# Weights in SBUF places of 16 KB a partition, experts' weights in transfers of 2 MB

## The chip, the cores and the metric

The kernel runs on one core of a Trainium2 chip. The metric is the device time of one execution in microseconds (us). TensorE (PE) does the matmuls, VectorE (DVE) and ScalarE (ACT) the elementwise work, GpSimd (POOL) a few scans, and SyncE (SP) issues nearly all loads from HBM to SBUF. SBUF has 128 partitions; "8 KB a partition" is 1 MB in all. Sixteen DMA engines move the data.

## The reference

Three blocks work in a chain on one input `x` of 256 tokens by 1024 features, all in float32. The first has two layers of feed-forward networks (width 2816) around a mixer. The second has attention and then a mixture of 32 experts. The third has attention beside a state-space branch, a cross-attention to a memory of 1024 features, and a feed-forward network with a convolution. The experts are what the change is about. The reference, cut to that:

```python
def moe_ffn(h, w_router, b_router, w_mlp1, b_mlp1, w_mlp2, b_mlp2):
    logits = (xf @ w_router + b_router).astype(jnp.float32)
    top_val, top_idx = lax.top_k(logits, TOP_K)          # 4 of 32 experts
    gates = jax.nn.softmax(top_val, axis=-1)
    ...
    def expert_block(args):
        xb, e = args
        hid = xb @ w_mlp1[e] + b_mlp1[e]                 # 1024 x 2048
        glu = jnp.minimum(hid[..., ::2], SWIGLU_LIMIT)
        lin = jnp.clip(hid[..., 1::2], -SWIGLU_LIMIT, SWIGLU_LIMIT)
        act = glu * jax.nn.sigmoid(SWIGLU_ALPHA * glu) * (lin + 1.0)
        return act @ w_mlp2[e] + b_mlp2[e]               # 1024 x 1024
    ...
    y = y * slot_gate[:, None].astype(y.dtype)
    out = jax.ops.segment_sum(y, slot_tok, num_segments=n + 1)[:n]
```

An expert has 8 MB in `w_mlp1` and 4 MB in `w_mlp2`. All 32 experts get tokens, so 384 MB are read for them; the whole kernel reads 705 MB.

## The kernel before

The activations stay in SBUF in transposed form (`xT`: features on partitions, 8 blocks of 128 features by 256 tokens). A weight outside the experts is loaded into a place of 8 KB a partition, split by ACT (L181, `hi`) and DVE (L182, `lo`) into a high and a low part, and used by three matmuls each (`mm3`, L198 to L200). The splits go through a ring of 8 tiles, the loads through a pool of 10 places (`rawp`). `slot` (L311) hands out the next place of that pool, `raw` (L314) loads into it (L318). When a place is asked for again, the load waits until all readers of what lay there are done. SP issues the loads in the order of the program, so a load that waits holds up all that stand behind it.

The experts are used without the split. `moe` (L1264) takes them one by one in an order that the router gives. `weights` (L1299) issues 12 loads of 1 MB for each expert at L1294. Feature `8p + u` of the expert's input lies with partition `p`, so row `u` of `w_mlp1` is one contiguous piece of 8 KB for each partition (2048 numbers), and rows `u` and `u + 1` are neighbours in HBM. Of `w_mlp2` one load takes two rows of 1024 numbers, again 8 KB. The places for these loads come in a fixed cycle of 16 (L1284): seven of `rawp`, four of a pool of its own (`wb`), two that are lent (`input` and `xT`, which the experts don't need; `xT` is kept in HBM meanwhile and loaded back at L1776), and three of `rawp`. The first expert's last row goes to `xe`. The matmuls with `w_mlp1` stand at L1516 (half a block of tokens) and L1548 (a full one), those with `w_mlp2` at L1590; L1563 and L1575 turn the activations between them, L1603 adds the result into the output. A transfer counts on one of eight semaphores in turn, and a load waits until the transfer before it on the same semaphore has landed, so that eight are under way at most. At three turns of the loop, weights and memory for the third block's cross-attention are loaded in between (`mem.fetch`), and a loop at L1781 for experts with more tokens than the turns allow for runs no round here.

Of the kernel before, what the change touches and what calls it, by code (L numbers as in the profile page):

```python
# [12 lines left out]
F32 = mybir.dt.float32  # L13
# [6 lines left out]
P = 128  # L20
T = 256
D = 1024
KT = D // P
# [18 lines left out]
class Net:  # L42
    def __init__(self, ctx, tc, I):
        self.ctx, self.tc, self.nc, self.I = ctx, tc, tc.nc, I
        self.uid = 0
        pool = lambda name, bufs, **kw: ctx.enter_context(tc.tile_pool(name=name, bufs=bufs, **kw))
        self.const = pool("const", 1)
        self.psum = pool("psum", 8, space=PSUM)
        self.small = pool("small", 2)
        self.rawp = pool("rawp", 10, reuse_waits="tile")  # L50
        self.inputs = pool("inputs", 2, reuse_waits="tile")
        self.ring_size, self.ring_scope, self.right_scope, self.latest = None, None, None, ()
        self.rings(8)
        nc = self.nc
        self.ident = self.const.tile([P, P], F32, name="ident")
        make_identity(nc, self.ident)
        self.ones = self.const.tile([P, 1], F32, name="ones")
        nc.vector.memset(self.ones, 1.0)
        self.mhalf = self.const.tile([P, 4], F32, name="mhalf")
        nc.vector.memset(self.mhalf, -0.5)  # L60
        self.sc = self.const.tile([P, KT], F32, name="sc")
        self.xT = self.const.tile([P, KT, T], F32, name="xT")
        self.new_inputs()
# [86 lines left out]

    def load_x(self, ap):
        nc = self.nc
        xin = self.rawp.tile([P, 2, D], F32, tag="raw", name=self.nm("xin"))
        for q in range(2):
            c = slice(512 * q, 512 * q + 512)
            nc.sync.dma_start(xin[:, :, c], ap[:, c].rearrange("(h p) d -> p h d", p=P))
        for j in range(0, KT, 2):
            ps = self.bank()
            for z in range(2):
                for h in range(2):  # L160
                    nc.tensor.transpose(ps[:, z * T + h * P:z * T + (h + 1) * P], xin[:, h, (j + z) * P:(j + z + 1) * P], self.ident)
            nc.vector.tensor_copy(self.xT[:, j:j + 2, :].rearrange("p j t -> p (j t)"), ps)

    def store_x(self, ap):
        nc = self.nc
        for q in range(2):
            ot = self.rawp.tile([P, 2, 512], F32, tag="raw", name=self.nm("ot"))
            for h in range(2):
                ps = self.bank()
                for j in range(4):  # L170
                    nc.tensor.transpose(ps[:, j * P:(j + 1) * P], self.xT[:, 4 * q + j, h * P:(h + 1) * P], self.ident)
                if h:
                    nc.scalar.copy(ot[:, h, :], ps)
                else:
                    nc.vector.tensor_copy(ot[:, h, :], ps)
            nc.sync.dma_start(ap[:, q * 512:(q + 1) * 512].rearrange("(h p) d -> p h d", p=P), ot)
# [131 lines left out]
        return r[:, 0:2], r[:, 2:4]  # L308


    def slot(self, dtype=F32):  # L311
        return self.rawp.tile([P, 2048], dtype, tag="raw", name=self.nm("raw"))

    def raw(self, src, k, n, load=True):  # L314

# [5 lines left out]
    def unit(self, src, slot=False):  # L321

        hi, lo = self.parts(src.shape[1], src.shape[2], slot)
        self.latest = self.split(hi, lo, src)
        return hi, lo
# [944 lines left out]
    def moe(self, V, mod, router, w1, w2, b2, nxt, ahead, mem):  # L1270
# [5 lines left out]
        outer_pools, first_pools, first_products = ExitStack(), ExitStack(), ExitStack()  # L1276
        pool = lambda name, bufs=1, **side: outer_pools.enter_context(self.tc.tile_pool(name=self.nm(name), bufs=bufs, reuse_waits="tile", **side))
        top, p0, p6 = (pool(name, side="right") for name in ("mot", "mo0", "mo6"))
        p3, pb = pool("mo3", 4), pool("mob")

        own = lambda: p3.tile([P, 2048], F32, tag="wb", name=self.nm("wb"))


        lent = [self.input, lambda: self.xT.rearrange("p j t -> p (j t)")]  # L1284
        places = itertools.cycle([self.slot] * 7 + [own] * 4 + lent + [self.slot] * 3)

        def place(last=False):
            p = next(places)
            return next(q for q in itertools.chain([p], places) if not (last and q in lent))()

        def load(src, n, t):

            t = t.rearrange("p (k n) -> p k n", n=n)
            nc.sync.dma_start(t, src)  # L1294
            return t

        chosen_rows = lambda: px.tile([P, KT, T], F32, tag="xe", name=self.nm("xe")).rearrange("p k n -> p (k n)")

        def weights(a, b, other={}, late=False, last=False):  # L1299
            a = a.rearrange("(p k) n -> p k n", k=KT)  # L1300
            b = b.rearrange("(p k) n -> p k n", k=KT)
            if late:
                room = [self.slot() for _ in range(4)]
                return lambda u: load(a[:, u:u + 1, :], 2048, room[u % 4]), lambda u: load(b[:, 2 * u:2 * u + 2, :], D, room[u])
            wa = {u: load(a[:, u:u + 1, :], 2048, place(last)) for u in range(KT) if u not in other}
            wb = [load(b[:, 2 * u:2 * u + 2, :], D, place(last)) for u in range(4)]
            wa.update((u, load(a[:, u:u + 1, :], 2048, t())) for u, t in other.items())
            return wa, wb

# [21 lines left out]
        half = [r >= HALF or (c > 0 and ranks[c - 1] == r) for c, r in enumerate(ranks)]  # L1331
# [11 lines left out]
        b1 = pb.tile([P, 2, 512], F32R, name=self.nm("b1"))  # L1343
        nc.sync.dma_start(b1.bitcast(F32), self.b1)
        start = weights(w1[0], w2[0], {7: chosen_rows})
        tokens = self.input().rearrange("p (h k q) -> p h k q", h=2, k=KT)
        with self.tc.high_priority():
# [6 lines left out]
            with self.behind([self.powered]):  # L1354
# [5 lines left out]
                while c < N:  # L1360
                    r, n = ranks[c], 1
                    if r < FULL:
                        nc.gpsimd.memset(crow[:, c:c + 2], float(r))
                        nc.gpsimd.memset(skip[:, c + 1:c + 2], float(S))
                        n = 2
# [28 lines left out]
            for h in range(2):  # L1394
# [9 lines left out]
                last = nc.vector.tensor_scalar(mask[:, h, :], rep[:, :E], -2e38, None, op0=ALU.is_le).ins  # L1404
# [30 lines left out]
        last = nc.vector.tensor_scalar(perm, crow, rank[:, 1:2], None, op0=ALU.is_equal).ins  # L1435
# [6 lines left out]
        with self.behind([last]):  # L1442
            nc.vector.scalar_tensor_tensor(slot, pp[:, :2 * E].rearrange("p (h e) -> p h e", h=2), 1.0, mask, op0=ALU.add, op1=ALU.mult)

            for h in range(2):
                last = nc.vector.tensor_scalar(oh0[:, h, :], iot, 1.0, slot[:, h, 0:1], op0=ALU.add, op1=ALU.is_equal).ins
        with self.behind([last]):
            nc.vector.tensor_scalar(slot, slot, 1.0, None, op0=ALU.subtract)
            cnt = p0.tile([P, E], F32, name=self.nm("cnt"))
            nc.vector.tensor_copy(cnt, pp[:, 2 * E:3 * E])  # L1450
# [27 lines left out]
        with self.tc.tile_pool(name=self.nm("mo1"), bufs=1, reuse_waits="tile") as p1, \  # L1478
# [280 lines left out]
            for turn_, r in enumerate(order):  # L1759
                e = nc.sync.value_load(ids[0:1, c:c + 1], min_val=0, max_val=E - 1)  # L1760
                wa, wb = weights(w1[bass.ds(e, 1)].rearrange("o a n -> (o a) n"), w2[bass.ds(e, 1)].rearrange("o a n -> (o a) n"), last=turn_ == len(order) - 1)
                mine = [c, c + 1] if r < FULL else [c]
                c += len(mine)
                late = [n for n in range(3) if mem and turn_ == VALUES + 2 * n]
                for n in late:
                    mem.fetch("v", n)
                acts = first(mine, wa)
                if c < N and c not in got:
                    prepare(c)
                second(mine, [(turned_half if half[i] else turned)(a) for i, a in zip(mine, acts)], wb)  # L1770
                if turn_ == VALUES - 3:
                    bias()
                    ends, key, rest, at, eid, ecol4 = beyond()
                for n in late:
                    mem.value(n, lambda: p2.tile([P, 2, T], F32, tag="a", name=self.nm("mv")))
# [5 lines left out]
            with tc.For_i(0, count, 1):  # L1781
                who = p2.tile([P, 2], F32, tag="who", name=self.nm("who"))
                u = p2.tile([P, E], F32, tag="u", name=self.nm("u"))
# [4 lines left out]
                wa, wb = weights(w1[bass.ds(e, 1)].rearrange("o a n -> (o a) n"), w2[bass.ds(e, 1)].rearrange("o a n -> (o a) n"), late=True)  # L1788
# [4 lines left out]
                for h in range(2):  # L1793
                    u = p2.tile([P, E], F32, tag="u", name=self.nm("u"))
# [1082 lines left out]
```

## Time and profile before

| | us |
|---|---|
| median of 3 runs (lowest to highest) | 2651.24 (2647.99 to 2656.15) |
| the profiled execution | 2649.92 |
| its span in the trace | 2648.2 |
| PE busy in the span | 2416.1 (91%) |
| DVE busy, ACT busy | 1339.3 (51%), 915.4 (35%) |
| transfers for the experts, 1 MB each | 384 |

The profile divides the span into 40 slices of 66.2 us, counted from 0 here. The experts' work lies in slices 18 to 31 (about 1180 to 2130 us). The attention of the second block lies just before them, in slices 15 to 17, and the third block behind them. Line numbers are those of the kernel before. A list of waits gives the total in us, how often, and the longest. In a timeline, a row gives start, duration, engine, line, operation, tiles and count of merged instructions, and in brackets the idle time before with what ended it. A table of stretches gives the length, the busy time of PE, PEld (weight loads into TensorE), DVE, ACT and POOL with their counts of instructions, the mean granted clock of TensorE as a share of full speed, the mean busy share of the 16 DMA engines, and GB/s.

### The profile page before, as it was taken

The numbers are of one execution on the slowest core, as the hardware profiler recorded it, in microseconds if no ns is written. First come the engines' busy times: TensorE is split into PE (matmuls) and PEld (weight loads), VectorE is DVE, ScalarE is ACT, GpSimd is POOL, SyncE is SP. The second block draws the span as 40 slices with busy tenths as digits, with TensorE's granted clock in tenths as the row PEclk, the third lists the DMA queues.
The fourth block names the chain that finished last, engine by engine and source line by source line (L and its number), as shares of the span: only waits on it lengthen the run. The fifth ranks groups of instructions, "written<-read, shape, count | busy, mean of one in ns | idle before, by whom it ended". The sixth has DMA issues, their size and how long they took to land. (4 is left out here: it accounts for less than half of the span.)

```text
span 2648.2 us, 42809 instructions
## 1 busy us (share of the span) xinstructions
PE 2416.1 (91%) x17207; PEld 1833.3 (69%) x17207; DVE 1339.3 (51%) x2778; ACT 915.4 (35%) x1531; POOL 254.3 (10%) x444
## 2 busy tenths in 40 slices
PE   7999999999999998999988988888787688999998
PEld 7998999999989998783333433233232156899997
DVE  5556767577787766832112111111111059766875
ACT  4446454454454445531101101001010043555653
POOL 0011000110021003120000000000000027111000
PEclk9999999999999999989989999899898788999998
DMA  8965555676647652469999999999999973444640
GB/s 247 329 196 193 185 204 192 220 263 231 216 158 248 223 168 94 158 250 391 419 414 417 416 416 419 420 419 419 420 419 420 420 286 112 160 165 139 222 144 17
DMA packets 274405, 718.30 MB, mean 271 GB/s; under 512 B 15055, under 2 KB 179387, under 8 KB 223643
## 3 DMA queue, kind: packets, MB, share of 16 engines
q1 hardware_dynamic: 269658, 705.73, 71.3%
q0 software_dynamic: 4544, 9.80, 1.1%
q8 instruction: 136, 2.23, 0.3%
q14 instruction: 67, 0.54, 0.1%
HBM read 704.89 MB, written 10.59 MB: 270 GB/s over the span
## 5 line engine op out<-in xcount | busy, mean ns | idle before, releaser
L200 PE MATMUL b<-input,hi 128*128 128x256 f32 x2392 | 671.6, 281 | 16.2 <-DVE hi L182 16.1
L198 PE MATMUL b<-input,hi 128*128 128x256 f32 x2392 | 675.5, 282 | 6.4 <-ACT input L210 5.1
L182 DVE TENSOR_TENSOR hi<-raw,hi 128x1024 fp32r<-128x1024 f32 (+3 forms) x517 | 605.8, 1183 | 146.4 <-ACT hi L181 145.5
L199 PE MATMUL b<-input,hi 128*128 128x256 f32 x2392 | 670.6, 280 | 3.7 <-DVE input L211 2.4
L181 ACT CAST hi<-raw 128x1024 fp32r<-128x1024 f32 (+3 forms) x517 | 509.0, 1002 | 469.4 <-PE b L200 408.2
L198 PEld LDWEIGHTS b<-input,hi 128*128 128x128 f32 x2392 | 456.4, 191 | 20.1 <-ACT hi L181 7.2
L200 PEld LDWEIGHTS b<-input,hi 128*128 128x128 f32 x2392 | 455.4, 190 | 18.9 <-DVE hi L182 18.8
L199 PEld LDWEIGHTS b<-input,hi 128*128 128x128 f32 x2392 | 456.0, 191 | 5.8 <-DVE input L211 4.5
L1497 DVE TENSOR_SCALAR g<-b 128x256 f32<-128x256 f32 x48 | 20.3, 423 | 588.4 <-PE b L1516 327.7
L198 PE MATMUL b<-ahi,hi 128*128 128x256 f32 x1072 | 299.2, 280 | 2.2 <-ACT ahi L181 2.2
L199 PE MATMUL b<-alo,hi 128*128 128x256 f32 x1072 | 298.0, 278 | 3.3 <-DVE alo L660 1.9
L200 PE MATMUL b<-ahi,hi 128*128 128x256 f32 x1072 | 297.5, 278 | 0.8 <-DVE hi L182 0.8
L199 PEld LDWEIGHTS b<-alo,hi 128*128 128x128 f32 x1072 | 202.4, 189 | 4.4 <-DVE alo L182 2.2
L198 PEld LDWEIGHTS b<-ahi,hi 128*128 128x128 f32 x1072 | 202.0, 189 | 3.6 <-ACT ahi L181 3.6
L200 PEld LDWEIGHTS b<-ahi,hi 128*128 128x128 f32 x1072 | 202.0, 189 | 1.0 <-DVE hi L182 1.0
L1500 ACT ACTIVATE sg<-g 128x256 f32<-128x256 f32 x48 | 20.0, 417 | 516.8 <-DVE g L1497 516.8
L1548 PE MATMUL b<-raw,xe 128*64 128x512 f32 x600 | 140.9, 607 | 10.2 <-DMA raw<-in_w_mlp_dram 10.1
L1516 PE MATMUL b<-raw,xe 128*32 128x512 f32 x784 | 107.9, 660 | 32.9 <-DMA raw<-in_w_mlp_dram 32.9
L1597 ACT COPY y<-b 64x512 f32<-64x512 f32 x68 | 39.4, 580 | 253.9 <-PE b L1590 246.1
L474 DVE TENSOR_TENSOR t<-b,rb 128x256 f32<-128x256 f32 x88 | 37.1, 422 | 151.7 <-PE b L200 151.6
L1548 PEld LDWEIGHTS b<-raw,xe 128*64 128x64 f32 x600 | 39.8, 138 | 104.8 <-issue 73.8
L1516 PEld LDWEIGHTS b<-raw,xe 128*32 128x32 f32 x784 | 20.3, 113 | 106.6 <-DMA raw<-in_w_mlp_dram 67.8
(673 smaller groups left out, 3317.3 us busy)
## 6 DMA issues: line engine op xcount, KB each, us to landing
raw<-in_w_mlp_dram SPq DMA_DIRECT2D x241, 1024.0 KB
wb<-in_w_mlp_dram SPq DMA_DIRECT2D x96, 1024.0 KB
raw<-in_ffn_w_in_dram SPq DMA_DIRECT2D x84, 1024.0 KB
raw<-in_ffn_w_out_dram SPq DMA_DIRECT2D x44, 1024.0 KB
raw<-in_w_ada_dram SPq DMA_DIRECT2D x24, 1024.0 KB
input<-in_w_mlp_dram SPq DMA_DIRECT2D x23, 1024.0 KB
xT<-in_w_mlp_dram SPq DMA_DIRECT2D x23, 1024.0 KB
raw<-in_ffn_w_up_dram SPq DMA_DIRECT2D x22, 1024.0 KB
```

Of the source, the lines that this page charges most:

```text
L181: a = self.nc.scalar.copy(hi, src)
L182: return a.ins, self.nc.vector.tensor_tensor(lo, src, hi.bitcast(F32), op=ALU.subtract).ins
L198: mm(out, whi, xhi, start=start, stop=False, skip_group_check=True)
L199: mm(out, whi, xlo, start=False, stop=False, skip_group_check=True)
L200: mm(out, wlo, xhi, start=False, stop=stop, skip_group_check=True)
L474: nc.vector.tensor_tensor(t, ps[:, :T], rb, op=ALU.mult)
L1497: nc.vector.tensor_scalar(g, v[:, :, 0], 7.0, None, op0=ALU.min)
L1500: nc.scalar.activation(sg, g, AF.Sigmoid, scale=1.702)
L1516: mm(ps[32 * c:32 * c + 32, :], xe(k), chunk(w[k][:, 0, :], c), start=False, stop=k == KT - 1, tile_position=(0, 32 * c), skip_group_check ...
L1548: mm(pq[q][64 * b:64 * b + 64, :], xe(k), chunk(w[:, 0, :], 2 * q + b), start=False, stop=k == KT - 1, tile_position=(0, 64 * b), skip_gro ...
L1597: nc.scalar.copy(y[64 * z:64 * z + 64, 512 * c:512 * c + 512], py[64 * c:64 * c + 64, :])
```

## The change

The pool `rawp` has 5 tiles of 16 KB a partition in place of 10 of 8 KB. `pair` hands out such a tile. `slot` hands out halves: the second half of a pair goes to the next one who asks, unless three more pairs have been handed out meanwhile; then it stays unused. All users of `rawp` go through `slot` now, those that load the input and store the output too. The experts' own pool has 2 tiles of 16 KB in place of 4 of 8 KB. The cycle of places is now three pairs, two of their own, the lent two as one pair, and two pairs: as much SBUF as before. `load_two` loads two neighbouring rows of `w_mlp1` (or four of `w_mlp2`) with one transfer of 2 MB, in which each partition gets one contiguous piece of 16 KB. Where the lent pair is next, it makes two transfers of 1 MB, since `input` and `xT` are no neighbours. The first expert's row 6 and the last two loads of the last expert's `w_mlp2` go alone into halves. Line numbers move by 1 up to `slot`, by 12 behind it, by 7 at the experts' load and by 23 behind `weights`.

```diff
-        self.rawp = pool("rawp", 10, reuse_waits="tile")
+        self.rawp = pool("rawp", 5, reuse_waits="tile")
+        self.pairs, self.other = 0, {}
...
+    def pair(self, dtype=F32):
+
+        self.pairs += 1
+        return self.rawp.tile([P, 4096], dtype, tag="raw", name=self.nm("raw"))
+
     def slot(self, dtype=F32):
-        return self.rawp.tile([P, 2048], dtype, tag="raw", name=self.nm("raw"))
+
+        half, since = self.other.pop(dtype, (None, 0))
+        if half is not None and self.pairs - since < 3:
+            return half
+        t = self.pair(dtype)
+        self.other[dtype] = t[:, 2048:], self.pairs
+        return t[:, :2048]
...
-        p3, pb = pool("mo3", 4), pool("mob")
+        p3, pb = pool("mo3", 2), pool("mob")
...
-        lent = [self.input, lambda: self.xT.rearrange("p j t -> p (j t)")]
-        places = itertools.cycle([self.slot] * 7 + [own] * 4 + lent + [self.slot] * 3)
...
+        lent = lambda: (self.input(), self.xT.rearrange("p j t -> p (j t)"))
+        places = itertools.cycle([self.pair] * 3 + [own] * 2 + [lent] + [self.pair] * 2)
...
+        def load_two(src, n, last):
+
+            p = next(places)
+            t = next(q for q in itertools.chain([p], places) if not (last and q is lent))()
+            half = src.shape[1] // 2
+            if isinstance(t, tuple):
+                return [load(src[:, half * z:half * z + half, :], n, x) for z, x in enumerate(t)]
+            t = load(src, n, t)
+            return [t[:, half * z:half * z + half, :] for z in range(2)]
...
-            wa = {u: load(a[:, u:u + 1, :], 2048, place(last)) for u in range(KT) if u not in other}
-            wb = [load(b[:, 2 * u:2 * u + 2, :], D, place(last)) for u in range(4)]
+            wa = {}
+            for u in range(0, KT, 2):
+                if u + 1 in other:
+                    wa[u] = load(a[:, u:u + 1, :], 2048, self.slot())
+                else:
+                    wa.update(zip((u, u + 1), load_two(a[:, u:u + 2, :], 2048, last)))
+            wb = load_two(b[:, 0:4, :], D, last)
+            wb += [load(b[:, u:u + 2, :], D, self.slot()) for u in (4, 6)] if last else load_two(b[:, 4:8, :], D, last)
```

On SP's queue, in the attention of the second block and at the first expert, this stood before. A row is a line, an operation, and the tile that is written with what it is read from (`w_q_b`, `w_kv_b` and `w_o` are weights of that attention); a number behind `raw` names one place of the pool.

```order
L318 DMA raw_12629<-in_w_q_b_dram 128x2x768
L318 DMA raw_12741<-in_w_kv_b_dram 128x1024
L1160 DMA raw_13351<-in_w_o_dram 128x2x1024
L1160 DMA raw_13428<-in_w_o_dram 128x2x1024
L1163 DMA raw_13484<-in_w_o_dram 64x2x1024 x2
L1163 DMA raw_13517<-in_w_o_dram 64x2x1024 x2
L318 DMA raw_13533<-in_xa_wk_dram 128x8x256
L318 DMA raw_13761<-in_xa_wk_dram 128x8x256
L1294 DMA raw_13838<-in_w_mlp_2_dram 128x2048
L1294 DMA raw_13840<-in_w_mlp_2_dram 128x2048
L1294 DMA raw_13842<-in_w_mlp_2_dram 128x2048
L1294 DMA raw_13844<-in_w_mlp_2_dram 128x2048
```

The same loads on SP's queue now:

```order
L330 DMA raw_12521<-in_w_q_b_dram 128x2x768
L330 DMA raw_12521<-in_w_kv_b_dram 128x1024
L1172 DMA raw_13242<-in_w_o_dram 128x2x1024 x2
L1175 DMA raw_13374<-in_w_o_dram 64x2x1024 x4
L330 DMA raw_13422<-in_xa_wk_dram 128x8x256 x2
L1301 DMA raw_13726<-in_w_mlp_2_dram 128x4096
L1301 DMA raw_13728<-in_w_mlp_2_dram 128x4096
L1301 DMA raw_13730<-in_w_mlp_2_dram 128x4096
```

The order of the loads is the same, but two neighbours now lie in one place, and seven loads of the first expert have become three pairs and, further back, one single row.

On SP's queue where the second expert's loads begin (ISA rows set the address by the expert's number), before:

```order
L1294 DMA input_14198<-in_w_mlp_2_dram 128x2048
L1294 ISA
L1294 DMA xT<-in_w_mlp_2_dram 128x2048
L1294 ISA
L1294 DMA raw_14201<-in_w_mlp_2_dram 128x2048
L1294 ISA
L1294 DMA raw_14203<-in_w_mlp_2_dram 128x2048
L1294 ISA
L1294 DMA raw_14205<-in_w_mlp_2_dram 128x2048
```

And now:

```order
L1301 DMA input_14076<-in_w_mlp_2_dram 128x2048
L1301 ISA
L1301 DMA xT<-in_w_mlp_2_dram 128x2048
L1301 ISA
L1301 DMA raw_14079<-in_w_mlp_2_dram 128x4096
L1301 ISA
L1301 DMA raw_14081<-in_w_mlp_2_dram 128x4096
```

The lent places keep their two transfers of 1 MB; behind them one issue brings what two brought. Over the whole program SP issues 553 transfers in place of 720: 167 pairs stand where 334 rows stood. The matmuls keep their order nearly everywhere; ACT and DVE split some weights outside the experts in a slightly different order.

## Rows read from the trace of the kernel before

**Rows 1.** The span in 40 slices of 66.2 us: PE, DMA share, rate.
```profile
PE 7999999999999998999988988888787688999998
DMA  8965555676647652469999999999999973444640
GB/s 247 329 196 193 185 204 192 220 263 231 216 158 248 223 168 94 158 250 391 419 414 417 416 416 419 420 419 419 420 419 420 420 286 112 160 165 139 222 144 17
```
**Rows 2.** Stretches: busy us of PE to POOL, PEclk, DMA share, GB/s.
```profile
1600.00:1800.00 200.00, 169.37 (x848) 61.47 (x849) 32.10 (x95) 17.59 (x35) 0.00 (x0) 0.92 1.01 420
...
2000.00:2120.00 120.00, 85.66 (x470) 26.69 (x470) 11.27 (x32) 9.14 (x19) 0.00 (x0) 0.82 1.01 420
```
**Rows 3.** PE's waits, 1220 to 2128 (us, times, longest).
```profile
PE b L1516 <- DMA raw<-in_w_mlp_dram: 32.9, 29, 2.5
```
**Rows 4.** SP's waits, 1220 to 2128 (us, times, longest).
```profile
SPq L1294 <- DMA raw<-in_w_mlp_dram: 373.0, 197, 3.0
SPq L1294 <- DMA wb<-in_w_mlp_dram: 153.6, 81, 3.5
...
SPq L1294 <- PE b L1516: 17.8, 16, 7.2
```
**Rows 5.** Timeline of SP (start, duration, line, tiles, count), around 1503.
```profile
1503.34 20.16 SPq L1294 DMA_DIRECT2D raw<-in_w_mlp_dram  x8
```
**Rows 6.** Packets and the queue's share: 525:535, 195:205, 1600:1800 in turn.
```profile
DMA packets 2023, 2.12 MB, mean 212 GB/s; under 512 B 33, under 2 KB 2000, under 8 KB 2022
...
q1 hardware_dynamic: 2022, 2.10, 64.9%
...
DMA packets 1411, 2.83 MB, mean 283 GB/s; under 512 B 34, under 2 KB 34, under 8 KB 1410
...
q1 hardware_dynamic: 1410, 2.82, 81.1%
...
DMA packets 11514, 83.91 MB, mean 420 GB/s; under 512 B 1279, under 2 KB 1279, under 8 KB 1279
...
q1 hardware_dynamic: 11504, 83.77, 101.0%
```
**Rows 7.** Timeline of SP, first loads of the experts.
```profile
1097.08 34.55 SPq L1294 DMA_DIRECT2D raw<-in_w_mlp_dram  x7
...
1172.30 7.54 SPq L1294 DMA_DIRECT2D raw<-in_w_mlp_dram  x3
```
**Rows 8.** Stretches at the experts' start, columns as in rows 2.
```profile
1160.00:1210.00 50.00, 45.20 (x236) 29.23 (x237) 19.75 (x85) 10.40 (x26) 9.23 (x41) 0.86 0.87 332
1210.00:1260.00 50.00, 46.07 (x246) 17.75 (x243) 8.92 (x28) 5.37 (x11) 0.00 (x0) 0.97 1.01 417
```
**Rows 9.** SP's longest wait of the whole span.
```profile
SPq L318 <- DVE hi L182: 457.8, 108, 19.0
```
**Rows 10.** Timeline of SP, loads of the second block's attention.
```profile
1022.92 0.37 SPq L318 DMA_DIRECT2D raw<-in_w_q_b_dram  x1
...
1051.23 6.48 SPq L1160 DMA_DIRECT2D raw<-in_w_o_dram  x2
1069.20 3.29 SPq L1163 DMA_DIRECT2D raw<-in_w_o_dram  x4
```
**Rows 11.** Timeline of DVE and ACT, splits in that attention.
```profile
1058.84 1.23 DVE L182 TENSOR_TENSOR hi<-raw,hi 128x128 fp32r<-128x128 f32 x3
...
1088.10 1.20 DVE L182 TENSOR_TENSOR hi<-raw,hi 128x1024 fp32r<-128x1024 f32 x1
...
1092.49 2.99 ACT L181 CAST hi<-raw 128x1024 fp32r<-128x1024 f32 x3
```
**Rows 12.** Timeline of PE, last matmuls of the experts and the first behind them.
```profile
2128.02 1.06 PE L1590 MATMUL b<-raw,aTh 128*32 128x512 f32 x8 [0.59 <-DMA raw<-in_w_mlp_dram]
...
2139.96 2.50 PE L2589 MATMUL b<-raw,m2f 128*128 128x256 f32 x5 [6.46 <-SPq L1781]
```
**Rows 13.** Queues of the whole span (packets, MB, share of 16 engines).
```profile
q8 instruction: 136, 2.23, 0.3%
```

More of the change, by code (lines that the diff above doesn't have):

```diff
@@ L152, in load_x @@
         nc = self.nc
-        xin = self.rawp.tile([P, 2, D], F32, tag="raw", name=self.nm("xin"))
+        xin = self.slot().rearrange("p (h n) -> p h n", h=2)
         for q in range(2):
@@ L166, in store_x @@
         for q in range(2):
-            ot = self.rawp.tile([P, 2, 512], F32, tag="raw", name=self.nm("ot"))
+            ot = self.slot()[:, :D].rearrange("p (h n) -> p h n", h=2)
             for h in range(2):
@@ L1278, in moe @@
         top, p0, p6 = (pool(name, side="right") for name in ("mot", "mo0", "mo6"))
-        p3, pb = pool("mo3", 4), pool("mob")
-        own = lambda: p3.tile([P, 2048], F32, tag="wb", name=self.nm("wb"))
-        lent = [self.input, lambda: self.xT.rearrange("p j t -> p (j t)")]
-        places = itertools.cycle([self.slot] * 7 + [own] * 4 + lent + [self.slot] * 3)
-        def place(last=False):
-            p = next(places)
-            return next(q for q in itertools.chain([p], places) if not (last and q in lent))()
+        p3, pb = pool("mo3", 2), pool("mob")
+        own = lambda: p3.tile([P, 4096], F32, tag="wb", name=self.nm("wb"))
+        lent = lambda: (self.input(), self.xT.rearrange("p j t -> p (j t)"))
+        places = itertools.cycle([self.pair] * 3 + [own] * 2 + [lent] + [self.pair] * 2)
         def load(src, n, t):
```

## The prediction

> **What bounds the kernel now.** Read first the slices of the span. PE is at 9 tenths or more almost everywhere except in slices 18 to 31 (counted from 0), and there the DMA engines stand at 9 tenths or more and move 414 to 420 GB/s [rows 1]. So the kernel has two limits: outside these slices the matmuls, inside them the transfer of the experts' weights. The table of stretches says it again for the steady middle: DMA share 1.01 and 420 GB/s, while PE is busy 169 of 200 us between 1600 and 1800, and 86 of 120 us between 2000 and 2120 [rows 2]. The list of what PE waits for has the landing of weights at its head: 32.9 us on L1516 [rows 3]. SP's own list shows why more of them are not under way: nearly all its waiting at L1294 is for an earlier transfer to land (373.0 us and 153.6 us), little for a matmul to free a place (17.8 us on L1516) [rows 4]. Eight transfers of 1 MB issue in 20.16 us, one in 2.52 us [rows 5], which is exactly the engines' pace. From about 1210 to 2120 us the time is therefore bytes over rate. A change of the rate changes the end almost one for one, since PE has some 15% to spare there.
>
> **Term 1: the size of a piece.** A transfer is cut into the contiguous pieces that a partition gets. For an expert these are 8 KB now and 16 KB after. What does an engine need for a piece? Three stretches have nearly one size each [rows 6]:
> - 525 to 535: 2022 packets, 2.10 MB, 64.9% of 16 x 10 us. Nearly all are 1 KB: 103.8 us over 2022 packets, about 51 ns each.
> - 195 to 205: 1410 packets, 2.82 MB, 81.1%. Without the 34 under 512 B they are of 2 KB: 129.8 us over 1376, 94 ns.
> - 1600 to 1800: 11504 packets, 83.77 MB, 101.0% of 3200 us. 1279 are under 512 B, 10225 are of 8 KB: 3232 us over 10225, 316 ns.
>
> A straight line through 1 KB and 8 KB has a slope of (316 - 51) / 7 = 37.9 ns for each KB and a fixed part of 51 - 37.9 = 13 ns. Through 2 KB and 8 KB it is 37.0 ns a KB and 20 ns fixed. A piece of 16 KB saves one fixed part against two of 8 KB. A pair of rows (2 MB) is 128 pieces in place of 256, over 16 engines 8 fewer on each: 8 x 13 ns = 0.104 us for each pair, 2.1% of 5.04 us. By the program's order 167 pairs are loaded so, and 50 rows still alone (the lent places, the first and the last expert). Some 160 pairs fall into the full stretch: 160 x 0.104 = 17 us. With 20 ns it is 160 x 0.163 = 26 us. No row shows a weight piece over 8 KB, so the lower bound is nothing gained. I take 17 us, because the 1 KB and 8 KB stretches span the larger range and the line between them is least bent by the noise of one of them.
>
> The Trainium skill, "DMA: Bandwidth & Descriptors", section "Why small descriptors are slow (HBM only)", speaks of a fixed overhead of about 3 cycles for each packet. With the 850 MHz of its section "Where 436 GB/s comes from" that would be 3.5 ns, an estimate from that page, and the term would be 4.5 us. The rows above disagree on the size: they leave 13 to 20 ns, not 3.5.
>
> **Term 2: the start of the experts.** Here the change costs. A pair can be loaded only when both its halves are free, and SP issues in order. Now the first seven rows go out from 1097.08 in 34.55 us, and the first three rows of the next expert that go to `raw` from 1172.30 in 7.54 us [rows 7], each as soon as 8 KB are free. After, each of these issues waits for the later of two neighbours. The engines are not yet full in this stretch: their share is 0.87 between 1160 and 1210, so 50 x 0.13 = 6.5 us are idle, and 1.01 behind it [rows 8]. Idle time added here is not made up later, because every later microsecond is full. The first pair of the second expert waits for what the third of these rows waits for now, which is at most 7.5 us later than the first; `input` and `xT` go out just before and cover 5 us of that (two transfers of 2.52 us). The same pattern of 2 or 3 us of cover follows for the next pairs. I take 3 us, between 0 and 7.5. PE itself is not made late by it: it works on the first expert there, whose rows are still the first to go out.
>
> **Term 3: loads elsewhere.** Outside the experts the same 16 KB places serve all weights. Two loads that are neighbours in the program now go out together when the slower half is free. SP waits 457.8 us for DVE's splits at L182 [rows 9], so a load goes out when a place comes free, with the other nine filled or under way. At some 200 GB/s (185 to 263 in slices 2 to 8 [rows 1]) nine places of 1 MB are over 40 us of work, so a wait of 5 to 15 us is hidden by what has already landed. The exception is the attention of the second block. There `w_q_b` goes out at 1022.92, `w_o` from 1051.23 and its last four parts from 1069.20 [rows 10]. In the new order `w_q_b` and `w_kv_b` share one pair, and the last four parts of `w_o` another. Followed through the waits, the first goes out only at about 1054, and the last parts behind the split that DVE ends at 1088.10 + 1.20 = 1089.3, 20 us later than now. Landing takes some 3 us (2.52 us of moving and the issue): 1092.5, while ACT's splits of that weight run from 1092.49 [rows 11]. So these splits would start up to 3 us late, and ACT's work behind them with them. I take 2 us, between 0 and 9 for all such places together. For `w_q_b` I take nothing: it lands at about 1057, and DVE's halves of its splits, which PE needs too, begin at 1058.84 now [rows 11].
>
> At the end of the experts nothing is taken or given: the last expert keeps two single rows at its end, so the last landing (PE waits for it until 2128.02) still brings 1 MB, and the 6.46 us in which PE waits for SP at L1781 stay [rows 12]. That a landing now brings 2 MB makes PE wait 2.5 us longer for a first row and less for the second. It moves PE against the transfers, but not the transfers, since a free pair is still early: the places hold 16 MB, of which the engines need a few.
>
> **The sum.** -17 + 3 + 2 = -12 us. The profiled execution took 2649.92 us, which gives 2638; it lies 1.3 us under the median of the runs, so I forecast 2639.
>
> **The rivals.**
> - *No gain in rate.* The engines are full already (1.01), and a piece of 16 KB may be cut again or may take twice 316 ns. Only the costs stay: 2651 + 5 = 2656. For it: nothing in the trace shows a weight piece above 8 KB. Against it: the fixed part appears in all three sizes.
> - *Little gain.* The straight line bends on the way to 16 KB, and only half of the fixed part, 6.5 ns, is saved: 160 x 8 x 6.5 ns = 8 us, of which the costs leave 3: 2648. For it: the 2 KB stretch lies 5 ns above the line through the other two, so the line is not exact. Against it: the two lines give 13 and 20 ns, not less. The rule of the Trainium skill above, with its 4.5 us, would come out near here, at about 2652.
> - *More gain.* 20 ns a piece: -26 + 5, so 2630.
> - *Slower: places held too long in the attention.* If `w_q_b` comes 31 us later (1054.0 against 1022.92) and PE feels all of it, the price is 31 us: 2651 - 17 + 3 + 31 = 2668. It decides from the point where more than some 22 us of these delays reach PE (at -17 + 3). For it: all casts of the stretch stand in ACT's one queue, in front of the softmax's exponentials. Against it: DVE comes to `w_q_b` only at 1058.84.
> - *Slower pieces.* The only pieces of 16 KB in the trace are those of the instruction queue: 136 packets, 2.23 MB, 0.3% of 16 x 2648 us, about 0.93 us each [rows 13], against 0.63 for two of 8 KB. At that price a pair costs 8 x 0.3 = 2.4 us more, 160 of them 384 us: about 3035. Against it: another queue with another destination, whose single packets lie far apart.
>
> **How the numbers follow.** Forecast 0.40 (2632 to 2643). More gain 0.15. No gain 0.15. Little gain 0.14. Held places 0.14. Slow pieces 0.02. A difference of 0.3% (8 us) is about what a measurement of this kernel can tell from none. Faster by more than it: 0.40 + 0.15 = 0.55. Within it: 0.15 + 0.14 = 0.29. Slower: 0.16. The range from 2622 to 2660 leaves out the held places and the slow pieces, and holds the bounds of the other terms.
>
> **What would show it.** In the changed profile the rate in the full stretch should be about 429 GB/s at a DMA share still near 1.01, and a piece of 16 KB should take about 619 ns. The full stretch should begin some 3 us later and end 12 us earlier. PE's waits for landings should be fewer and longer. If the rate is still 420, term 1 is wrong. If PE shows new waits for DVE or ACT between 1050 and 1130, or if it falls behind in the first layers, term 3 is too small.

## The result and the profile after

| | before | after |
|---|---|---|
| median of 4 runs each (lowest to highest), us | 2651.76 (2647.99 to 2656.15) | 2627.72 (2621.16 to 2629.94) |
| the profiled execution, its span | 2649.92, 2648.2 | 2626.88, 2625.2 |

The ratio is 0.9907, with a 95% interval from 0.9894 to 0.992: faster by 24 us, 0.9%. The sign was forecast and the time lies in the range, but it is 11 us below the forecast of 2639. Lines have moved: L1516 is L1539 now, L1294 is L1301, L1548 is L1571, L1590 is L1613, L878 is L890, L181 and L182 are L182 and L183, L936 to L938 are L948 to L950, L1025 is L1037, L1033 is L1045.

The steady stretch first. These are the stretches between 1600 and 1800 and around the experts' start (columns as in [rows 2]; they answer to [rows 2, 8]), and the packets of the first ([rows 6]):

```profile
1600.00:1800.00 200.00, 166.47 (x844) 57.08 (x841) 27.53 (x84) 16.03 (x32) 0.00 (x0) 0.93 1.01 426
...
1160.00:1210.00 50.00, 49.21 (x230) 26.23 (x231) 12.91 (x55) 7.43 (x14) 0.61 (x1) 0.88 0.88 354
1210.00:1260.00 50.00, 44.73 (x240) 18.03 (x238) 8.57 (x27) 4.32 (x9) 0.00 (x0) 0.97 1.01 428
```
```profile
DMA packets 6570, 85.17 MB, mean 426 GB/s; under 512 B 731, under 2 KB 731, under 8 KB 731
...
q1 hardware_dynamic: 6561, 85.04, 100.4%
```

The rate is 426 in place of 420 GB/s, and the packets are 6561 in place of 11504. The trace counts one packet for each piece of a partition; the 731 under 512 B carry no weights. The lent places still take 8 KB pieces, so both sizes are in it. 6561 - 731 = 5830 pieces hold 85.04 MB, which is 10381 times 8 KB; that makes 4551 pieces of 16 KB and 1279 of 8 KB. The time is 1.004 x 3200 = 3213 us. Less 1279 x 316 ns for the small ones [rows 6], 2809 us are left over 4551: **617 ns for a piece of 16 KB**. Two of 8 KB took 632, so by the recorded times a piece saved is worth 15 ns. Both shares are above 100%, so recorded times overlap a little. Counted by the 3200 us that passed, 10225 pieces of 8 KB took 313 ns each before, and the 4551 of 16 KB take 615 ns now: a piece saved is worth 11 ns of time, an estimate from the same rows.

What waits for what, from 1220 to 2110: PE's list and SP's list (us, times, longest; they answer to [rows 3, 4]):

```profile
PE b L1539 <- DMA raw<-in_w_mlp_dram: 45.4, 17, 3.9
```
```profile
SPq L1301 <- DMA raw<-in_w_mlp_dram: 224.8, 68, 13.3
SPq L1301 <- PE b L1539: 105.9, 43, 9.0
SPq L1301 <- PE b L1613: 104.4, 32, 11.8
SPq L1301 <- DMA wb<-in_w_mlp_dram: 96.0, 27, 5.9
```

PE's waits at this line are fewer and longer (17 in place of 29, at most 3.9 us in place of 2.5). SP, which waited 17.8 us for L1516 before, now waits over 200 us for matmuls at two lines to give a place free. A pair is held until the slower of its halves has been used. The engines stay full all the same (1.01), but the places have become a limit that is near: see the runs without the lent places.

To see where the 24 us are, the start of the same matmul was taken from both timelines, after minus before:

| time in the kernel before, us | after - before, us | what lies ahead of it |
|---|---|---|
| 800 to 944 | -3.1 | first layers; a second execution of the changed kernel has -1.4 here, so this is not assigned |
| 962 | -11.7 | a wait for DVE at the routing weights, gone |
| 1030 | -8.0 | a new wait at the start of the second block's attention |
| 1081 | -11.5 | a wait of 3.0 us for DVE at L1025, gone |
| 1160 to 1250 | -12.3 | rest of the attention, start of the experts |
| 2140 | -24.5 | the experts |
| end | -23.0 | third block |

So half of the gain came in the experts, as forecast. The other half was there before they began, where the prediction had a loss of 2 us.

**The 8.6 us between 944 and 962.** ACT's and PE's timelines of before (start, us, engine, line, tiles):

```profile
943.90 1.06 ACT L2516 ACTIVATE raw<-raw 128x1024 fp32r<-128x1024 f32 x1 [7.18 <-DMA raw<-in_mem_dram]
944.86 0.18 ACT L2516 ACTIVATION_READ_ACCUMULATOR raw<-raw 128x1 f32 x1
945.08 1.06 ACT L2516 ACTIVATE raw<-raw 128x1024 fp32r<-128x1024 f32 x1
946.04 0.18 ACT L2516 ACTIVATION_READ_ACCUMULATOR raw<-raw 128x1 f32 x1
946.14 1.03 ACT L181 CAST hi<-raw 128x1024 fp32r<-128x1024 f32 x1
947.07 0.41 ACT L476 ACTIVATE s<-t 128x256 f32<-128x256 f32 x1
```
```profile
950.94 3.62 PE L878 MATMUL b<-raw,both 128*128 128x32 f32 x16 [4.34 <-DVE both L869]
```

L2516 squares the memory of the third block, work that is needed much later. It stands in ACT's queue ahead of a cast and of a gate (L476) of the running feed-forward network. Its load was issued at 935.00, so ACT stands still for 7.18 us with that work behind it. DVE has the same order: L264 waits there for L2516. PE runs dry, and when it goes on the granted clock is at half, as the stretches of before show:

```profile
950.00:955.00 5.00, 4.06 (x19) 4.06 (x19) 4.85 (x25) 0.59 (x2) 0.00 (x0) 0.50 0.01 3
955.00:960.00 5.00, 5.00 (x26) 4.94 (x26) 1.48 (x12) 0.26 (x1) 1.30 (x2) 0.53 0.21 52
```

And after, ACT, PE and a stretch:

```profile
940.69 1.04 ACT L182 CAST hi<-raw 128x1024 fp32r<-128x1024 f32 x1
944.98 0.19 ACT L891 COPY b_route<-b 128x32 f32<-128x32 f32 x1 [3.25 <-PE b L890]
945.54 0.26 ACT L894 COPY raw<-b 16x128 f32<-16x128 f32 x1 [0.37 <-PE b L893]
947.88 1.06 ACT L2539 ACTIVATE raw<-raw 128x1024 fp32r<-128x1024 f32 x1 [2.09 <-DVE both L2041]
```
```profile
943.08 1.86 PE L890 MATMUL b<-raw,both 128*128 128x32 f32 x16
```
```profile
941.00:945.00 4.00, 4.00 (x36) 3.90 (x35) 3.85 (x22) 0.76 (x2) 0.00 (x0) 1.00 1.05 365
```

The squares (L2539 now) stand behind the cast and behind both copies of `route`, PE doesn't wait, and its sixteen matmuls take 1.86 in place of 3.62 us at the full clock. No edit names these lines. The planner, which orders the instructions of ACT and DVE when the program is built, gave them another order with the new places.

**The step between 1041 and 1081.** Here the lead grows from 8.0 to 11.5 us. DVE's timeline and PE's wait of before, and the stretch behind it:

```profile
1052.51 6.08 DVE L182 TENSOR_TENSOR hi<-raw,hi 128x512 fp32r<-128x512 f32 x4 [0.37 <-ACT hi L181]
1058.50 0.41 DVE L1033 TENSOR_TENSOR rt<-b,raw 128x256 f32<-128x256 f32 x1
```
```profile
PE b L1025 <- DVE rt L1033: 3.0, 1, 3.0
```
```profile
1060.00:1065.00 5.00, 4.80 (x20) 3.78 (x19) 5.00 (x19) 1.71 (x6) 0.00 (x0) 0.50 0.32 130
```

And after, DVE:

```profile
1041.82 1.28 DVE L183 TENSOR_TENSOR hi<-raw,hi 128x512 fp32r<-128x512 f32 x2
1043.02 0.42 DVE L1045 TENSOR_TENSOR rt<-b,raw 128x256 f32<-128x256 f32 x1
```

Four splits stood right ahead of L1033 on DVE, PE waited for it and ran at half clock afterwards; now two stand there, and PE doesn't wait at this line.

### The profile page after: what moved, and what is told of

Its sections match the earlier page's. It is cut to its first block, busy times and chain, and to the rows that moved or that the text cites. A ratio compares the mean times of both kernels' runs of the same rounds, so it can differ in the third digit from the quotient of the medians.

```text
span 2625.2 us, 42043 instructions
## 1 busy us (share of the span) xinstructions
PE 2388.1 (91%) x17207; PEld 1825.1 (70%) x17207; DVE 1337.9 (51%) x2778; ACT 914.8 (35%) x1531; POOL 250.2 (10%) x444
## 5 line engine op out<-in xcount | busy, mean ns | idle before, releaser
L182 ACT CAST hi<-raw 128x1024 fp32r<-128x1024 f32 (+3 forms) x517 | 510.3, 1002 | 492.8 <-PE b L201 418.6
L183 DVE TENSOR_TENSOR hi<-raw,hi 128x1024 fp32r<-128x1024 f32 (+3 forms) x517 | 603.4, 1177 | 152.1 <-ACT hi L182 150.2
L1539 PE MATMUL b<-raw,xe 128*32 128x512 f32 x784 | 110.2, 680 | 45.4 <-DMA raw<-in_w_mlp_dram 45.4
L1571 PE MATMUL b<-raw,xe 128*64 128x512 f32 x600 | 138.8, 607 | 12.5 <-DMA raw<-in_w_mlp_dram 12.4
L1571 PEld LDWEIGHTS b<-raw,xe 128*64 128x64 f32 x600 | 40.9, 139 | 105.5 <-issue 82.7
L1539 PEld LDWEIGHTS b<-raw,xe 128*32 128x32 f32 x784 | 23.0, 116 | 116.6 <-DMA raw<-in_w_mlp_dram 63.8
```

The lines of the kernel that those rows point to most:

```text
L182: a = self.nc.scalar.copy(hi, src)
L183: return a.ins, self.nc.vector.tensor_tensor(lo, src, hi.bitcast(F32), op=ALU.subtract).ins
L1539: mm(ps[32 * c:32 * c + 32, :], xe(k), chunk(w[k][:, 0, :], c), start=False, stop=k == KT - 1, tile_position=(0, 32 * c), skip_group_check ...
L1571: mm(pq[q][64 * b:64 * b + 64, :], xe(k), chunk(w[:, 0, :], 2 * q + b), start=False, stop=k == KT - 1, tile_position=(0, 64 * b), skip_gro ...
```

## The experiments

The kernels below were timed in three groups; each group has the kernel before beside it, at 2648.86, 2650.48 and 2648.07 us.

### One change alone: pairs filled by 1 MB transfers

```diff
-            t = load(src, n, t)
-            return [t[:, half * z:half * z + half, :] for z in range(2)]
+            return [load(src[:, half * z:half * z + half, :], n, t[:, 2048 * z:2048 * z + 2048]) for z in range(2)]
```

> The changed kernel, but each pair is filled by two transfers of 1 MB with pieces of 8 KB; places and order stay as changed. Theory (the gain in the experts' stretch comes from the 16 KB piece, 617 ns against 2 x 315 ns; the other half comes from the order of work before the experts): 12 to 14 us slower than the changed kernel, 2640, about 12 us faster than before; rate in the full stretch 420 GB/s. Rival (all of the 24 us comes with the transfers): 2652, as before. Rival (all of it comes with the places and the order): 2628, as changed.

Measured: 2640.46 us, ratio 0.9959 (0.9943 to 0.9975). The stretch from 1600 to 1800 is that of before again:

```profile
1600.00:1800.00 200.00, 169.13 (x848) 58.83 (x846) 31.32 (x93) 17.25 (x35) 0.00 (x0) 0.92 1.01 420
```

Against before, the matmuls start 12.0 us earlier at 1201 and 11 us earlier at 2165: all of the gain ahead of the experts is there, and nothing is won within them. The step to 0.9907 of the full change, 0.5% or 14 us by the ratios and 13 us by the medians, is what the transfers of 2 MB bring.

### Transfers of 2 MB with pieces of 8 KB

```diff
-        return self.rawp.tile([P, 4096], dtype, tag="raw", name=self.nm("raw"))
+        return self.rawp.tile([P, 4104], dtype, tag="raw", name=self.nm("raw"))
...
-        own = lambda: p3.tile([P, 4096], F32, tag="wb", name=self.nm("wb"))
+        own = lambda: p3.tile([P, 4104], F32, tag="wb", name=self.nm("wb"))
...
-            t = load(src, n, t)
-            return [t[:, half * z:half * z + half, :] for z in range(2)]
+            t = t.rearrange("p (z m) -> p z m", z=2)[:, :, :2048]
+            nc.sync.dma_start(t, src.rearrange("p (z k) n -> p z (k n)", z=2))
+            return [t[:, z, :].rearrange("p (k n) -> p k n", n=n) for z in range(2)]
```

The second half of a place begins 32 B later, so a partition's piece is cut in two; the second halves that `slot` hands out begin at 2056 too.

> The changed kernel with 32 bytes left free between the two halves of each place of 16 KB: still one transfer of 2 MB, but each partition gets two pieces of 8 KB. Theory (the size of the piece counts): the rate falls to 420 GB/s, a piece takes 315 ns, 2640. Rival (the number of transfers and of their completions counts): the rate stays at 426 GB/s, 2628.

Measured: 2646.19 us, ratio 0.9986 (0.9977 to 0.9996). The stretch from 1600 to 1800 and its packets:

```profile
1600.00:1800.00 200.00, 163.66 (x832) 56.62 (x830) 29.26 (x87) 16.44 (x33) 0.00 (x0) 0.94 1.01 421
```
```profile
DMA packets 10995, 84.22 MB, mean 421 GB/s; under 512 B 721, under 2 KB 721, under 8 KB 721
...
q1 hardware_dynamic: 10986, 84.09, 101.0%
```

The transfers are as few as in the changed kernel (the packets under 512 B are 721, against 731 there and 1279 before), the pieces are as small as before, and the rate is 421. A piece takes 1.010 x 3200 us over 10265, 315 ns as before, so the shift by 32 B isn't seen to cost anything. So it is the piece that counts for the rate, not the number of transfers; fewer transfers are worth 1 of the 6 GB/s at most. The time isn't the 2640 that was expected. This kernel also lost some 7 us behind the experts, in the third block, at a mean clock of 0.95 in place of 0.97 between 2300 and 2500. Why this is so was not followed.

### The order alone: before, with the memory's squares behind the routing copies

```diff
-        nc.scalar.copy(row[:2 * KT, 0:P], ps[:2 * KT, P:2 * P])
+        self.routed = nc.scalar.copy(row[:2 * KT, 0:P], ps[:2 * KT, P:2 * P]).ins
...
-            nc.scalar.activation(m2[0][:, 0:4, :].rearrange("p j t -> p (j t)"), min_[:, h, :], AF.Square, accum_out=ms[:, h:h + 1])
+            with net.behind([net.routed]):
+                nc.scalar.activation(m2[0][:, 0:4, :].rearrange("p j t -> p (j t)"), min_[:, h, :], AF.Square, accum_out=ms[:, h:h + 1])
```

> The kernel before, with one thing changed: ACT's two squares of the memory (L2516) may only come behind ACT's copies for the router (L879, L882), as in the changed kernel. Theory (8.6 of the 12 us before the experts were ACT's wait for the memory's load, behind which the last splits of the feed-forward network stood, and the half clock after it): 8 to 9 us faster than before, 2643, PE's wait of 4.3 us on L878 gone. Rival (these 12 us come from the places or from the clock of that run): within 3 us of before, 2650.

Measured: 2639.06 us, ratio 0.9956 (0.9942 to 0.9971). ACT's and PE's timelines now read as those of after do:

```profile
947.69 0.25 ACT L882 COPY raw<-b 16x128 f32<-16x128 f32 x1 [0.37 <-PE b L881]
947.85 1.05 ACT L2517 ACTIVATE raw<-raw 128x1024 fp32r<-128x1024 f32 x1
```
```profile
945.23 1.86 PE L878 MATMUL b<-raw,both 128*128 128x32 f32 x16
```

The step between 944 and 961 is -8.6 us, as in the changed kernel; 3.7 of it are given back between 1021 and 1081; a lead of 6.1 us remains behind the experts (at 2165), 7.7 at the end. So the order of one group of instructions, with the old places and the old transfers (419 GB/s), makes the kernel faster. By the ratios it brings what the kernel with 1 MB transfers brought (0.9959), and 0.9956 and the 0.5% of the pieces add up to the whole. By the timelines it does not bring all of it: at 2165 that kernel is 11 us ahead of before. They part between 1041 and 1081, where the wait at L1025 is still there:

```profile
PE b L1025 <- DVE rt L1033: 2.9, 1, 2.9
```

So this second gain goes with the places (the changed kernel and the one with 1 MB transfers, which have the new ones, lack the wait), but no run moves these splits alone.

### Without the lent places

```diff
-        places = itertools.cycle([self.pair] * 3 + [own] * 2 + [lent] + [self.pair] * 2)
+        places = itertools.cycle([self.pair] * 3 + [own] * 2 + [self.pair] * 2)
```

> The changed kernel without the lent places in the cycle: seven pairs (14 MB) in place of eight, and all but a few rows in transfers of 2 MB (190 pairs in place of 167). Theory (piece size, and the places hold more than the engines need): 23 more pairs at 0.1 us each, 2 to 3 us faster than the changed kernel, 2625, rate 428 GB/s. Rival (after the change the places set how far the loads run ahead, so one place fewer leaves the engines idle at times): 5 to 20 us slower than the changed kernel, DMA share below 1.0 in the stretch.

Measured: 2629.75 us, ratio 0.9937 (0.992 to 0.9954). Three stretches of it:

```profile
1160.00:1200.00 40.00, 39.21 (x210) 21.61 (x210) 14.28 (x65) 7.43 (x14) 0.69 (x1) 0.98 0.80 316
1450.00:1475.00 25.00, 25.00 (x116) 12.06 (x116) 0.84 (x3) 3.28 (x6) 0.52 (x1) 1.00 0.87 362
1600.00:1800.00 200.00, 164.63 (x851) 57.73 (x850) 30.70 (x92) 17.77 (x36) 0.00 (x0) 0.96 1.01 427
```

Every piece has 16 KB now, and the steady rate rises by 1 GB/s. But between 1450 and 1475 the engines have idle time, which the changed kernel doesn't have there (1.01, 428 GB/s): PE is busy all of the 25 us, and places come free late. The theory's gain is not there. The rival named the cause, but its 5 to 20 us are not shown: this median is 2 us above that of the changed kernel, and the two intervals of the ratio touch.

### Towards a faster version

Six runs, to see whether the rest is to be had. First the changed kernel again, on the chip of the next three.

> The changed kernel once more, so that the next three stand beside it on one chip. Every theory: about 2628 us, 0.991 of the kernel before, 426 GB/s between 1600 and 1800.

Measured: 2627.08 us, ratio 0.9916 (0.9901 to 0.9931).

Then the lent places in the first four turns alone:

```diff
-        places = itertools.cycle([self.pair] * 3 + [own] * 2 + [lent] + [self.pair] * 2)
+        round_ = [self.pair] * 3 + [own] * 2 + [lent] + [self.pair] * 2
+        places = itertools.chain(round_ * 4, itertools.cycle([p for p in round_ if p is not lent]))
```

> The changed kernel, with the two lent places (input and xT) taken in the first four turns of the places only, and left out of the turns behind them. Theory: the lent places are worth their 1 MB transfers at the start of the experts, where the run without them showed idle DMA engines (share 0.80 between 1160 and 1200, 389 GB/s between 1450 and 1500), and cost rate in the steady stretch, where that run moved 427 against 426 GB/s. So with them early only: 427 GB/s between 1600 and 1800, no idle engines at the start, and about 2 us less than the changed kernel (2626). Rival: two places fewer make SP wait more often for matmuls wherever it is, the engines fall idle in the later turns as well, and the time is 2628 to 2632.

Measured: 2631.07 us, ratio 0.9921 (0.9904 to 0.9939). The theory fell by a wrong count: four turns are 64 MB, used up long before 1450, and the hole there was deeper than without any lent places. The time is the rival's:

```profile
1450.00:1475.00 25.00, 25.00 (x126) 12.36 (x128) 0.85 (x3) 3.27 (x6) 0.70 (x1) 1.00 0.73 303
```

Next, the loss at 1013 to 1030. In the changed kernel two splits for later columns stand on DVE ahead of the first `xlo`; DVE's timeline, PE's waits from 1000 to 1060 and a stretch:

```profile
1013.41 3.19 DVE L183 TENSOR_TENSOR hi<-raw,hi 128x1024 fp32r<-128x1024 f32 x2
1016.53 0.87 DVE L950 SCALAR_TENSOR_TENSOR input<-h,mod,input 128x256 fp32r<-128x256 f32 x2
```
```profile
PE b L200 <- DVE input L950: 2.2, 1, 2.2
```
```profile
1015.00:1020.00 5.00, 2.94 (x14) 2.94 (x14) 5.00 (x7) 1.65 (x3) 2.79 (x3) 0.51 1.09 368
```

```diff
-                nc.vector.scalar_tensor_tensor(self.xlo[:, j, :], h, ...)
+                done = nc.vector.scalar_tensor_tensor(self.xlo[:, j, :], h, ...)
+            done = done.ins
...
-                nc.scalar.copy(qi[:, i, :], product(wide((1184 + i * P, P))))
+                with self.behind([done]):
+                    unit = wide((1184 + i * P, P))
+                nc.scalar.copy(qi[:, i, :], product(unit))
```

The same was done with the groups at 928 and 1056.

> The changed kernel, with the splits of the four column groups 928 to 1440 of the second block's w_in put behind the last of the eight xlo (L950) on ACT and DVE. Theory: in the changed kernel two of these splits (3.19 us of DVE from 1013.41) stand ahead of the first xlo, PE waits 2.2 and 1.9 us for input and runs at half clock between 1015 and 1020, and some 4 us of the 8.6 won before are lost there. Put behind, the loss at 1013 to 1025 goes: 2624, a step of about -4 between 1010 and 1030 that stays. Rival: DVE has as much to do in that stretch either way, so PE waits for these splits at the product of columns 1184 instead and nothing remains at 1081: 2628.

Measured: 2626.1 us, ratio 0.9906 (0.9888 to 0.9925). PE's wait for L950 fell from 2.2 to 0.2 us, and beside the changed kernel of the same chip PE started 2.4 us earlier at 1160. Of these, 1.3 us were left at 1445 and 0.6 us at 2135. The edit does what it says. Why the lead shrinks is open: the first load of the experts goes out 1.8 us earlier as well (1104.37 against 1106.15), and two executions of the changed kernel differ by 1.6 us at 2165, so a lead of this size can't be followed further here.

> Both of the two edits before it on the changed kernel. Theory: they lie in different stretches, so the gains add: about 2622 (-4 before the experts and -2 in them). Rival: an earlier start of PE gives nothing, because the experts' loads start no earlier and bytes over rate set the end of that stretch: 2626 to 2628.

Measured: 2628.24 us, ratio 0.9914 (0.9899 to 0.9929). Beside the changed kernel of the same chip PE was 5.9 us ahead at 1160 (2.5 of them already in the first layers), 3.8 behind the hole at 1450 to 1475, and 1.6 us at the end. In the hole (0.82, 339 GB/s) the engines lose some 25 x 0.19 = 4.8 us. The time is the rival's, but its reason is not: the experts' loads do start earlier (1100.83 against 1106.15), and the missing lent places take much of it back.

The last two runs, on another chip, have `round_ * 11` in place of `round_ * 4`, first without and then with the edit of the splits.

> As the run with the lent places in the first four turns, but in the first eleven turns. That run moved 427 GB/s in the steady stretch but had idle engines at 1450 to 1475 (share 0.73, 303 GB/s), where the changed kernel has 1.01: four turns are 64 MB, which are used up by about 1270, so the lent places were missing there. Theory: SP waits there for matmuls to free places, the changed kernel's loads to input at 1436.41 and xT at 1436.93 bring the 2 MB that bridge it, and eleven turns (176 MB) reach behind it. So a share of 1.01 between 1450 and 1475, then 427 GB/s, and 2625 to 2626. Rival: the hole moves to another place behind the last turn with lent places, since every stretch in which PE is the slower one empties the places: again 2629 to 2631.

Measured: 2627.2 us, ratio 0.9921 (0.9906 to 0.9935). The hole is closed and the steady rate is 427:

```profile
1450.00:1475.00 25.00, 25.00 (x146) 15.80 (x146) 0.85 (x3) 3.27 (x6) 0.70 (x1) 1.00 1.01 428
...
1600.00:1800.00 200.00, 166.50 (x855) 57.23 (x855) 27.35 (x84) 17.18 (x34) 0.00 (x0) 0.93 1.01 427
```

So the hole was the lack of lent places there, as the theory had it, and it did not move elsewhere. The time is that of the changed kernel all the same, and the 1 to 2 us that the theory expected are less than these runs can show.

> The splits behind L950 as before, and the lent places in the first eleven turns. Theory: the start of PE and of the experts' loads some 2.5 us earlier is kept as long as no hole takes it back; with the hole at 1450 to 1475 bridged the end comes 3 to 5 us before that of the changed kernel: about 2623. Rival: what PE wins before the experts is given back in the full stretch as in the run with the splits alone, where 2.6 us at 1041 were 0.6 at 2135 beside the changed kernel on that chip: 2626 to 2628.

Measured: 2623.86 us, ratio 0.9899 (0.9881 to 0.9916). It is the lowest median of all, but its interval overlaps that of the changed kernel (0.9894 to 0.992): not shown to be faster.

## Why the prediction was right, and where it was not

- **Term 1, the size of a piece (-17 us): right in mechanism, a little large.** The fixed part was there: 617 ns were measured for 16 KB, 619 were forecast, and the piece that is saved is worth 15 ns, between the 13 and the 20 of the two lines. At 160 pairs that is 160 x 8 x 15 ns = 19 us. But the step took recorded times of packets for time that passes, at a share that stays as it was. The share went from 101.0 to 100.4% of 16 engines, and 0.6% of some 890 us are 5 us. With the 11 ns of time that passed it is 160 x 8 x 11 ns = 14 us. The bytes moved in 200 us say the same: 85.04 against 83.77 MB is 1.5%, of 890 us 13 us. The rate was 426, not 429. That 8 KB pieces in 2 MB transfers gave 421 settles that the piece is the cause.
- **The rule weighed there.** The Trainium skill, "DMA: Bandwidth & Descriptors", section "Why small descriptors are slow (HBM only)", has about 3 cycles of fixed overhead for a packet, from which the prediction estimated 3.5 ns. The trace doesn't agree on the size: it shows 15 ns for a piece, 11 by the time that passed.
- **Term 2, the start of the experts (+3 us): in its bounds, nearer to zero.** The stretch from 1160 to 1210 has a share of 0.88 (0.87 before), and the next is full in both. The experts as a whole brought 12.2 us (from -12.3 to -24.5), against 13 from the rate, which leaves about 1 us for the start; no row separates it further. The first load of the experts does go out later, at 1106.48 against 1097.08, though PE is 12 us earlier.
- **Term 3, loads elsewhere (+2 us): wrong in sign.** This is the step that failed. It looked at SP alone and asked only which loads come later. They do: `w_q_b` goes out at 1043.13 and the last parts of `w_o` at 1083.49, though PE is 8 to 12 us earlier there. It cost nothing that can be seen. What was left out, and so put at nothing, is that new places also give ACT and DVE another order, though the section on the change had noted that they split some weights in another order. That moved the squares of the memory behind the routing copies and took away a wait of 4.3 us with the half clock behind it (-8.6 us), and the wait of 3.0 us at L1025 is gone (the lead grows by 4.4 us between 1041 and 1160). In between, from 962 to 1030, 3.7 us of lead are lost (1.6 in the second execution). The two splits ahead of `xlo` are part of that, 2.0 us by the run that puts them behind; but the run with the order alone, where one split stands there as before, loses 1.8 us in the same stretch. The wait of 7.18 us on ACT stood in the trace of before, outside the stretches that the prediction read. The run with the order alone, in the old places, shows its worth: 0.9956. So the time came out below the forecast by something that nobody had planned. The terms that the prediction did argue come to -12 us, as it forecast; that the rest made the kernel faster and not slower, and that the time still lies in the range, is luck.
- **The end of the experts (0): right, but for the places.** PE waits 6.19 us for SP at L1804 now, against 6.46 at L1781 [rows 12]:

```profile
2115.42 6.47 PE L2612 MATMUL b<-raw,m2f 128*128 128x256 f32 x16 [6.19 <-SPq L1804]
```

That a free pair is still early, as this step held, is true only just: SP waits 210 us for matmuls at two lines now, and with 14 MB of places in place of 16 the engines fall idle at 1450.

- **The rivals.** No gain in rate: it would leave the rate at 420 GB/s, as in the kernel with 1 MB transfers; it is 426. Little gain: its 6.5 ns a piece are too few against 11. More gain (2630) came nearest to the time, but for another reason: its 20 ns a piece are not there. The time of 2628 lies outside the 2632 to 2643 that had the largest chance. Held places in the attention: between 1050 and 1130 PE waits only 1.3 us for DVE and none for ACT. Slow pieces: 617 ns, not 930.
- **The sum.** -13 in the rate, +1 at the start, some -12 before the experts, +1.5 behind them: about -23, the difference of the two profiled executions. The -12 are -3.1 in the first layers (-1.4 in a second execution), -8.6 for the squares, +3.7 until 1030 and -4.4 from there to 1160.

## What to carry to other kernels

Where the transfers set the time and their engines are full, the longest contiguous piece for each partition is worth having: read the time of a piece from stretches with one size each, and check the gain by the bytes that move in a fixed time: of the 15 ns that the recorded times gave, 11 came back here. When a change alters places or sizes that a planner works with, look at the order that it gives every engine, and search the whole trace of before for waits that another order would remove or make, not just the loads. Time that PE wins ahead of a stretch that is bound by transfers is to be judged behind that stretch: of 12.0 us in the kernel with 1 MB transfers 11 were left there, but of the small leads of the later runs (2.4 and 5.9 us) only 0.6 and 3.4.

## What the runs showed of the hardware that was not expected

- By the recorded times a DMA piece has a fixed part of about 15 ns beside some 37 ns for each KB, up to 16 KB a partition. 2 MB transfers with pieces of 8 KB moved 421 GB/s, with pieces of 16 KB alone 427 (without the lent places), and 1 MB transfers with pieces of 8 KB 420.
- Behind a wait of PE of 4.34 us the granted clock was 0.50 and 0.53 for the next two stretches of 5 us, that is mostly the lower of the two levels. Sixteen small matmuls took 3.62 us there and 1.86 us at the full clock. So PE's wait cost about twice its own length, 8.6 us. Behind the wait of 3.0 us at L1025 the clock was 0.50 too.
